# A backward-weight matmul with pair products: two more tiles taken as pairs, one accumulator set kept in three banks, closings and additions moved between engines

## The chip, the cores and the metric

The kernel runs on one core of a Trainium2 chip. The metric is the device time of one execution in microseconds; the median of three runs is given, and one further execution was profiled. In the profile PE is TensorE, PEld its weight loads, DVE VectorE, ACT ScalarE, POOL GpSimd and SP SyncE.

## The reference

```python
batch, m, k, n = 16, 512, 1024, 768
input:       (16, 512, 1024) float32
grad_output: (16, 512, 768)  float32
grad_weight = np.einsum('bmk,bmn->kn', input, grad_output)   # (1024, 768) float32
```

Seen as matrices, X is 8192 x 1024, G is 8192 x 768, and the output is X transposed times G: a contraction over 8192 rows.

## The kernel before

**Tiles.** The 8192 rows are 32 tiles of 256 rows, loaded one after another by POOL's queue (L152, L153; the first ones in halves, L157 and L159), with a conversion to bf16 on the way. Rows 0 to 127 of G and rows 0 to 255 of X come as float32 by SP's and ScalarE's queues and are rounded by VectorE and ScalarE (`round_by`, L199 to L217). `PAIRS_HELD` is the number of buffers that the tiles turn through, `SUMS_HELD` that of the sums below. All load instructions stand ahead of everything else that POOL does.

**Plain tiles and pairs.** `LOADS` says how each tile is used. The output is cut into four blocks: A (left columns, first half of k), B (right columns, first half), C (left, second half), D (right, second half), each of four row groups q = 0..3 of 128 x 384. A plain tile ("s") is two items of 128 rows; each item gives one matmul to each of the 16 groups, so a tile takes 32 matmuls. A pair tile ("P") is multiplied by a Winograd scheme for 2 x 2 blocks: seven products instead of eight, named 1, A, B, C, 5, 6 and 7, so 28 matmuls. The products need sums of the halves of X and of G: `sum_x` (L179, three VectorE operations) and `sum_g` (L189, three more), in the order written in the plan as x0.u, x1.u, x2.u and g0.u, g1.u, g2.u for tile u. At the end the shared products 1, 5, 6 and 7 are added into A, B, C and D (`SHARED`).

**Banks.** PSUM has eight banks of 512 float32 columns, and a group takes 384 of one bank. There are 32 groups (eight streams of four), so most groups are in PSUM only now and then. A group is *opened* by a matmul that starts it in a bank (`C3@5.1`: group C3 in bank 5, one matmul) or by a *fill* (`fD0@2`: ScalarE copies the group's sum so far from SBUF into the bank, L274). It is *closed* by ScalarE (`cC3`: copy to SBUF, L327) or VectorE (`vC2`: a copy, L329, or an addition to the sum in SBUF, L331, when the group was opened without a fill). The last closing of a group is done by VectorE and adds the shared product (L307 to L312), and the finished block is stored (L316 to L321), the first three in halves. A's four groups stay in banks 7, 3, 4 and 1 from start to end; banks 0, 2, 5 and 6 turn among all the others. The very last group, B3, is filled into two banks (`fB3@2+7`), as 256 and 128 columns.

**Order.** `PLAN` is one list, written out by hand or by a program outside the kernel, and the loop at L336 issues its tokens in that order. Each engine runs its own share of the list in order; what an engine waits for are the semaphores of the tiles that it touches. `WARMUP` (L133) is a handful of matmuls on constants ahead of the first data.

Of the kernel before, what the change touches and what calls it, by code (L numbers as in the profile page):

```python
# [9 lines left out]
P = 128  # L10

LOADS = "ssssssPPPPPPPPPPPPPPPPPPPPPPPPPs"

PLAN = (
    "A0@7.1 A3@3.1 A1@4.1 C3@5.1 C2@0.1 C1@2.1 r0 cC3 C0@6.1 vC2 A2@1.1 cC1 D0@5.1 vC0 B0@0.1 cD0 D1@2.1 "
    "r1 r3 B3@6.1 r2 D3@5.2 vB0 r4 A1.1 A2.1 cD1 vB3 A3.1 B1@0.2 cD3 B2@2.2 vB1 D2@6.2 cB2 C0@5.1 C1@0.1 "
    "vD2 A0.1 fD0@2 A2.1 vC0 A3.1 fD1@6 A1.1 D0.2 vC1 C2@5.2 cD0 D1.2 vC2 C3@0.2 cD1 B0@2.2 vC3 B3@5.3 "
    "fB1@6 vB0 A0.2 fB2@0 vB3 B1.2 fC0@2 B2.2 cB1 C1@5.2 vB2 C0.2 fD2@6 A3.1 vC1 D3@0.2 cC0 D2.2 fC2@5 "
    "vD3 C3@2.1 A1.1 cD2 A2.1 vC3 C2.1 B0@0.1 D1@6.1 vC2 D0@2.1 vB0 fD2@5 A3.2 vD1 A1.2 fB0@0 D2.2 vD0 "
    "B1@6.2 cD2 B0.2 vB1 B2@2.2 cB0 B3@5.2 vB2 C0@6.2 fC1@0 A2.2 vB3 fC2@2 C1.2 vC0 C3@5.2 cC1 C2.2 vC3 "
    "fD0@6 A0.2 D1@0.4 vC2 D3@5.4 vD1 D0.4 vD3 C3@2.2 vD0 B3@5.2 C0@0.2 vC3 fC1@6 A3.2 vB3 fB2@2 A0.2 vC0 "
    "C1.2 fD2@5 B2.2 cC1 D2.2 vB2 C2@0.2 cD2 B0@6.2 vC2 fB1@2 A1.4 vB0 fC1@0 B1.4 C2@5.2 cB1 D2@6.2 vC2 "  # L30
    "C1.2 fD0@2 A2.4 vD2 fD3@5 vC1 fC3@6 D0.2 D3.2 vD0 C3.2 cD3 C0@0.2 vC3 B2@2.4 vC0 fB3@6 B0@5.4 vB2 "
    "fD1@0 B3.4 fC0@2 vB0 A3.1 g0.6 fB1@5 A3.3 vB3 A0.2 g1.6 A0.2 fC1@6 D1.1 g2.6 D1.3 A2.2 vD1 A1.3 x0.6 "
    "fC2@0 C0.3 C1.1 x1.6 C1.2 cC0 C2.1 x2.6 C2.2 cC1 C3@2.1 g0.7 C3.2 cC2 B1.3 fD0@6 vC3 D2@0.2 g1.7 cB1 "
    "D0.2 vD2 fD3@2 A2.1 A3.1 A0.1 g2.7 cD0 10@5.1 D3.2 c10 x0.7 11@0.2 cD3 12@6.2 v11 13@5.2 c12 50@2.1 "
    "x1.7 50.1 c13 51@0.2 x2.7 52@6.2 c50 g0.8 53@5.2 c51 70@2.2 v52 c53 A2.1 g1.8 A3.1 fB3@0 72@6.2 v70 "
    "73@5.2 c72 g2.8 B3.2 v73 63@2.2 cB3 B2@6.1 x0.8 B2.1 fC1@5 A1.2 v63 A0.2 71@0.1 x1.8 71.2 vB2 62@2.3 "
    "c71 x2.8 C1.2 c62 g0.9 60@6.3 cC1 61@2.1 g1.9 61.2 fB0@0 v60 10@5.2 c61 g2.9 B0.3 v10 fC3@6 C2@2.2 "
    "cB0 x0.9 C2.1 C3.3 fC0@5 vC2 A2.2 f52@0 C0.1 x1.9 cC3 C0.2 A3.1 x2.9 A3.1 cC0 12@2.1 g0.10 12.1 52.2 "
    "f63@5 v12 B1@6.3 c52 g1.10 63.2 f13@2 vB1 11@0.2 c63 A0.1 g2.10 13.2 v11 72@5.2 c13 x0.10 A1.2 f51@0 "
    "53@6.2 v72 A0.1 f70@2 A3.1 51.1 x1.10 f50@5 51.2 v53 70.3 c51 x2.10 50.2 f73@6 g0.11 50.1 B3@0.3 c70 "  # L40
    "v50 73.2 fB2@2 g1.11 73.1 vB3 A2.1 f10@5 B2.2 c73 g2.11 B2.1 10.1 x0.11 10.2 cB2 C1@0.3 c10 x1.11 "
    "62@6.2 f71@2 vC1 A3.1 A1.1 f61@5 A0.1 x2.11 71.2 f60@0 g0.12 71.1 61.3 v62 c71 60.1 g1.12 60.2 c61 "
    "B0@2.1 g2.12 fB1@6 B0.2 v60 11@5.2 vB0 B1.2 fC0@0 A2.1 x0.12 A2.1 cB1 A0.1 C0.3 fC2@2 v11 A3.1 fC3@6 "
    "A1.1 x1.12 C2.3 cC0 x2.12 13@5.2 f53@0 g0.13 13.1 C3.3 cC2 v13 53.2 f52@2 g1.13 53.1 vC3 12@5.3 c53 "
    "g2.13 52.3 f72@6 v12 63@0.2 x0.13 c52 63.1 72.3 f62@5 v63 A2.1 f51@2 A1.1 x1.13 62.2 c72 51.1 x2.13 "
    "51.2 f50@0 v62 73@6.3 c51 g0.14 50.3 f70@5 v73 A3.1 fB2@2 A0.1 70.1 g1.14 c50 70.2 g2.14 B3@6.3 c70 "
    "B2.1 x0.14 B2.2 10@5.3 vB3 cB2 C1@0.1 x1.14 C1.2 f60@6 v10 11@2.3 x2.14 60.2 f61@5 g0.15 60.1 A1.1 "
    "61.3 c60 vC1 A0.1 g1.15 71@6.3 c61 v11 B0@0.1 fB1@5 g2.15 B0.2 v71 A2.2 fC2@2 A3.1 x0.15 A3.1 f52@6 "
    "B1.3 vB0 C2.2 cB1 x1.15 C2.1 52.2 cC2 x2.15 52.1 C0@0.1 fC3@5 g0.16 C0.2 A1.1 c52 A0.1 vC0 C3.3 "
    "f12@2 g1.16 13@6.3 vC3 12.2 g2.16 f62@5 12.1 v13 53@0.3 c12 x0.16 62.3 f72@6 A1.1 v53 63@2.3 c62 "  # L50
    "x1.16 f50@0 72.4 v63 f51@5 50.1 g0.17 50.2 c72 70@2.1 x2.16 70.2 c50 g1.17 51.3 v70 73@6.2 g2.17 c51 "
    "73.1 B2@0.1 x0.17 fB3@2 B2.2 A2.2 fC1@5 v73 B3.3 x1.17 C1.3 vB2 cB3 10@6.2 x2.17 cC1 10.1 71@0.1 "
    "g0.18 f11@2 71.2 A3.2 v10 f60@5 11.1 g1.18 11.2 v71 60.3 c11 g2.18 61@6.3 c60 x0.18 A0.3 fC0@2 v61 "
    "B1@0.3 fB0@5 x1.18 C0.3 fC2@6 vB1 B0.2 cC0 x2.18 B0.1 C2.1 g0.19 f12@0 C2.2 C3@2.3 cB0 vC2 12.2 "
    "f62@5 g1.19 12.1 vC3 A1.2 c12 53@6.1 g2.19 53.2 f52@2 x0.19 13@0.4 v53 A3.2 52.1 x1.19 f72@6 52.3 "
    "v13 62.2 x2.19 c52 62.2 g0.20 73@0.3 c62 g1.20 63@2.4 f51@5 v73 72.1 g2.20 72.2 fC1@0 v63 51.3 c72 "
    "x0.20 A2.3 c51 70@2.1 x1.20 70.3 f71@5 x2.20 50@6.4 v70 C1.1 g0.21 C1.2 fB2@2 A0.2 v50 cC1 B2.2 "
    "g1.21 B2.2 fB3@6 g2.21 A1.2 cB2 B3.4 x0.21 71.3 cB3 B0@0.2 x1.21 c71 B0.1 10@6.2 x2.21 10.2 vB0 "
    "C2@2.2 g0.22 C2.1 f61@0 A3.2 vC2 11@5.3 g1.22 11.1 f60@2 61.4 v10 g2.22 60.4 v11 c61 x0.22 C0@6.4 "
    "f53@0 c60 12@5.1 x1.22 12.3 vC0 B1@2.2 x2.22 B1.2 g0.23 C3@6.4 v12 53.2 g1.23 53.2 vB1 A1.2 c53 vC3 "  # L60
    "52@5.3 f73@2 g2.23 13@0.2 x0.23 13.2 A2.3 v52 A0.1 x1.23 A0.2 f51@5 v13 A3.2 51.1 x2.23 51.2 g0.24 "
    "51.1 73.3 c51 g1.24 73.1 C1@6.1 g2.24 C1.2 c73 63@5.4 vC1 f72@2 70@0.1 x0.24 f71@6 70.2 72.5 v63 v70 "
    "f62@5 A1.2 x1.24 c72 71.2 g0.25 71.2 f50@0 62.1 x2.24 fB2@2 62.2 g1.25 62.2 c71 B2.1 g2.25 B2.3 c62 "
    "50.4 vB2 B0@6.1 x0.25 f10@2 B0.3 c50 C2@5.1 x1.25 C2.3 f11@0 vB0 10.2 x2.25 10.2 g0.26 11.4 c10 vC2 "
    "B3@6.2 f60@2 g1.26 B3.2 c11 g2.26 B3.1 60.4 vB3 fB1@0 61@5.2 fC0@6 x0.26 61.2 c60 B1.4 v61 12@2.1 "
    "x1.26 fC3@5 12.3 vB1 C0.2 g0.27 f53@0 C0.2 x2.26 C3.2 cC0 g1.27 C3.2 v12 53.3 cC3 g2.27 53.1 52@6.4 "
    "v53 A2.1 x0.27 f51@0 A2.3 v52 A3.3 x1.27 A3.1 f70@6 A0.2 x2.27 A0.2 g0.28 A1.3 13@2.1 g1.28 13.2 "
    "g2.28 13.1 C1@5.4 v13 51.4 f73@2 vC1 70.1 x0.28 f63@5 70.3 c51 73.1 x1.28 73.3 c70 x2.28 73.1 63.2 "
    "c73 g0.29 63.3 f72@2 50@0.1 g1.29 50.2 c63 g2.29 50.1 71@6.4 v50 f62@5 72.4 fB0@0 v71 62.1 x0.29 "
    "f11@6 62.3 c72 B0.1 x1.29 B0.3 c62 x2.29 11.4 fB2@2 vB0 fC2@5 B2.1 g0.30 B2.4 f10@0 v11 C2.4 vB2 "  # L70
    "f11@6 10.1 g1.30 f12@2 10.3 vC2 A2.1 g2.30 A2.2 c10 x0.30 12.4 f13@5 f10@0 x1.30 11.1 13.3 c12 v11 "
    "10.1 A3.1 f61@2 x2.30 A3.2 v13 f62@6 A1.3 v10 f63@5 61.5 f60@0 62.2 v61 60.5 v62 f71@2 A2.2 f72@6 "
    "v60 A3.2 A1.2 vA2 f70@0 A0.5 vA3 vA1 70.3 vA0 63.2 v70 f50@1 71.2 72.2 fC0@3 v63 50.2 f73@0 v71 C0.6 "
    "f51@4 v72 fC1@5 v50 51.3 f52@2 fC2@7 C1.5 vC0 fD0@6 v51 fB0@1 52.4 fD1@3 B0.4 vC1 fB1@4 C2.3 v52 "
    "fD2@5 B1.7 vB0 fB2@2 vC2 73.2 vB1 B2.3 v73 f53@1 D0.2 D1.2 fC3@4 vB2 53.4 vD0 C3.6 vD1 v53 fD3@0 "
    "fB3@2+7 D2.2 D3.2 vC3 B3.7 vD2 vD3 vB3 "
).split()


WARMUP = [("b", 512), ("f", 512), ("f", 512), ("b", 512)]  # L80
PAIRS_HELD = 14
SUMS_HELD = 10

MERGED = 2


@with_exitstack
def kernel(
# [6 lines left out]
    nc = tc.nc  # L95
    bf16 = mybir.dt.bfloat16
    f32 = mybir.dt.float32
# [153 lines left out]


    SHARED = {"A": "1", "B": "5", "C": "7", "D": "1", "6": "1", "7": "6"}

    done = {(p, q): 0 for p in streams for q in range(Q)}
    fresh = {(p, q): True for p in streams for q in range(Q)}
    closed = set()
    opened = {}
    used = {7}
# [5 lines left out]
    def fill(p, q, b, b2):  # L265
        assert (p, q) not in opened and not fresh[p, q] and b in used
        src = sum_of(p, q)
        if b2 is None:
            parts = [(bank(b), 0, NH)]
        else:  # L270
            assert b2 in used
            parts = [(bank(b), 0, 256), (bank(b2), 256, NH)]
        for tile_, c0, c1 in parts:
            nc.scalar.copy(out=tile_[:, 0 : c1 - c0], in_=src[:, c0:c1])  # L274
        opened[p, q] = (parts, True)

    def multiply(p, q, b, n):
        first = (p, q) not in opened
        if first:
            opened[p, q] = ([(bank(b), 0, NH)], False)  # L280
            used.add(b)
        parts, carried = opened[p, q]
        for tile_, c0, c1 in parts:
            for j in range(n):
                at = done[p, q] + j
                stat, mov = operands(p, streams[p][at], q)
                nc.tensor.matmul(  # L287
                    tile_[:, 0 : c1 - c0],
                    stat,
# [7 lines left out]
    def close(engine, p, q):  # L297
# [34 lines left out]
        if final:  # L332
            closed.add((p, q))
# [51 lines left out]
```

## Time and profile before

| | us |
|---|---|
| median of 3 runs | 162.35 (162.25 to 162.43) |
| profiled execution | 162.31 |
| its span, first to last instruction | 160.5 |
| TensorE busy | 155.3, 937 instructions |
| VectorE busy | 142.7, 323 instructions |
| ScalarE busy | 112.8, 253 instructions |
| load queue (q0) | 28.64 MB, 90.2% of 16 engines' span |

The time is that of the whole execution; the span lies 1.8 us inside it. "Busy" is the time in which at least one of the engine's instructions ran. The instructions of one engine overlap in its pipeline, so what one of them costs is better read from the distance between two starts than from its own duration. Two lines give the sizes of the main copies; after the count stand the busy time, the mean duration in ns, and the idle time of the engine just before them:

```profile
L274 ACT COPY bank<-macc 128x384 f32<-128x384 f32 x71 | 33.6, 484 | 13.2 <-DVE macc L331 5.6
L327 ACT COPY macc<-bank 128x384 f32<-128x384 f32 x61 | 28.6, 479 | 9.5 <-PE bank L287 8.1
```

### The profile page before, as it was taken

To read this page: it belongs to the slowest core of one execution; us is meant where nothing else is said; L and a number is where in the kernel's file an instruction comes from. 1 tells how busy PE (TensorE), PEld (TensorE's weight loads), DVE (VectorE), ACT (ScalarE), POOL (GpSimd) and SP (SyncE) were. 2 spreads that over 40 slices of the span, in tenths; PEclk is the share of its full clock that TensorE was granted. 3 is DMA by queue.
4 is the path that set the end of the run, shared out by engine and by line. 5 is a ranking of instruction groups with operands and counts; after the bars stand their busy time and mean duration, and the time that the engine had idled before them with its cause. 6 is when DMAs were issued, how large, how long until landed. Compare 5 with 4: busy or idle time off the path is not lost.

```text
span 160.5 us, 2776 instructions
## 1 busy us (share of the span) xinstructions
PE 155.3 (97%) x937; PEld 91.9 (57%) x937; DVE 142.7 (89%) x323; ACT 112.8 (70%) x253; POOL 34.8 (22%) x69
## 2 busy tenths in 40 slices
PE   8899999999999999999999999999999999999990
PEld 3355556556556656655655655665665665556560
DVE  0788986989999999999989998998899998989992
ACT  3779737749888999968777786534777368877730
POOL 7452222122221222222122222212222100000000
PEclk9999999999999999999999999999999999999999
DMA  5999999999999999999999999999999999924385
GB/s 176 295 213 213 210 216 213 213 213 212 213 212 212 213 213 214 210 214 213 215 214 213 213 212 212 213 212 214 213 210 213 215 212 214 212 43 157 137 294 196
DMA packets 12830, 33.40 MB, mean 208 GB/s; under 512 B 1424, under 2 KB 4624, under 8 KB 12816
## 3 DMA queue, kind: packets, MB, share of 16 engines
q0 software_dynamic: 9360, 28.64, 90.2%
q1 hardware_dynamic: 3024, 3.47, 6.3%
q10 hardware_dynamic: 432, 1.11, 1.8%
q8 instruction: 7, 0.11, 0.3%
q14 instruction: 7, 0.06, 0.1%
HBM read 58.72 MB, written 3.15 MB: 385 GB/s over the span
## 4 chain that ended last, share of the span: by engine, by line
DMA 48%; PE 44%; DVE 2%; issue 2%; POOL 1%; DVEq 0%; POOLq 0%
DMA xp<-in_input_dram 48%; PE bank L287 44%; POOL gp L157 1%; DVE acc L312 1%; DVE xe L183 0%; POOL xp L159 0%; DVE acc L331 0%; DVE macc L331 0%; DVEq L380 0%; DVE xe L185 0%; POOLq L153 0%; POOLq L369 0%; POOLq L152 0%
## 5 line engine op out<-in xcount | busy, mean ns | idle before, releaser
L287 PE MATMUL bank<-gp,xp 128*128 128x384 bf16 (+2 forms) x631 | 109.8, 324 | 0.6 <-DVE xp L201 0.6
L287 PEld LDWEIGHTS <-xp 128*128 128x128 bf16 x631 | 61.1, 98 | 42.5 <-DVE xp L201 1.3
L287 PE MATMUL bank<-ge,xe 128*128 128x384 bf16 x300 | 56.2, 326 | 0.1
L274 ACT COPY bank<-macc 128x384 f32<-128x384 f32 x71 | 33.6, 484 | 13.2 <-DVE macc L331 5.6
L287 PEld LDWEIGHTS <-xe 128*128 128x128 bf16 x300 | 29.3, 98 | 19.9 <-issue 0.6
L274 ACT COPY bank<-acc 128x384 f32<-128x384 f32 (+1 forms) x70 | 32.3, 479 | 9.1 <-DVE acc L329 5.5
L327 ACT COPY macc<-bank 128x384 f32<-128x384 f32 x61 | 28.6, 479 | 9.5 <-PE bank L287 8.1
L331 DVE TENSOR_TENSOR acc<-bank,acc 128x384 f32<-128x384 f32 x54 | 28.7, 552 | 2.8 <-PE bank L287 1.2
L153 POOL DMA_DIRECT2D xp<-in_input_dram x30 | 16.0, 532 | 53.3 <-DMA xp<-in_input_dram 28.0
L327 ACT COPY acc<-bank 128x384 f32<-128x384 f32 x45 | 21.4, 480 | 6.5 <-PE bank L287 6.0
L152 POOL DMA_DIRECT2D gp<-in_grad_output_dram x30 | 16.0, 533 | 37.1 <-DMA gp<-in_grad_output_dram 15.0
L331 DVE TENSOR_TENSOR macc<-bank,macc 128x384 f32<-128x384 f32 x41 | 22.5, 551 | 0.5 <-PE bank L287 0.2
L183 DVE TENSOR_TENSOR xe<-xp 128x1024 bf16<-128x1024 bf16 x25 | 17.1, 683 | 1.2 <-DMA xp<-in_input_dram 1.2
L329 DVE COPY acc<-bank 128x384 f32<-128x384 f32 x24 | 13.1, 553 | 3.0 <-PE bank L287 2.4
L193 DVE TENSOR_TENSOR ge<-gp 128x768 bf16<-128x768 bf16 x25 | 13.8, 550 | 0.0
L187 DVE TENSOR_TENSOR xp<-xp,xe 128x512 bf16<-128x512 bf16 x25 | 10.5, 419 | 0.4
L185 DVE TENSOR_TENSOR xe<-xe,xp 128x512 bf16<-128x512 bf16 x25 | 10.5, 418 | 0.3
L197 DVE TENSOR_TENSOR gp<-ge,gp 128x384 bf16<-128x384 bf16 x25 | 8.8, 352 | 0.3
L195 DVE TENSOR_TENSOR ge<-gp,ge 128x384 bf16<-128x384 bf16 x25 | 8.7, 350 | 0.2
L312 DVE TENSOR_TENSOR acc<-bank,macc 128x384 f32<-128x384 f32 (+2 forms) x17 | 8.0, 522 | 0.0
L329 DVE COPY macc<-bank 128x384 f32<-128x384 f32 x14 | 7.6, 552 | 0.4 <-PE bank L287 0.4
L201 DVE CAST gp<-gf 128x192 bf16<-128x192 f32 (+1 forms) x2 | 0.7, 360 | 4.9 <-DMA gf<-in_grad_output_dram 4.9
(17 smaller groups left out, 21.6 us busy)
## 6 DMA issues: line engine op xcount, KB each, us to landing
xp<-in_input_dram POOLq DMA_DIRECT2D x30, 512.0 KB, 16.9
gp<-in_grad_output_dram POOLq DMA_DIRECT2D x30, 384.0 KB, 16.7
out_dram<-acc SPq DMA_DIRECT2D x12, 192.0 KB, 1.9
xf<-in_input_dram ACTq DMA_DIRECT2D x2, 512.0 KB, 5.0
gp<-in_grad_output_dram POOLq DMA_DIRECT2D x3, 192.0 KB, 6.6
out_dram<-acc SPq DMA_DIRECT2D x6, 96.0 KB, 1.7
xp<-in_input_dram POOLq DMA_DIRECT2D x2, 256.0 KB, 8.0
gf<-in_grad_output_dram SPq DMA_DIRECT2D x2, 192.0 KB, 4.2
```

Of the source, the lines that this page charges most:

```text
L152: nc.gpsimd.dma_start(out=gp, in_=G[rows, :].rearrange("(p m) n -> p m n", m=2))
L153: nc.gpsimd.dma_start(out=xp, in_=X[rows, :].rearrange("(p m) k -> p m k", m=2))
L183: nc.vector.tensor_sub(out=xe[:, 0:2, :], in0=x[:, 1::-1, :], in1=x[:, 3::-2, :])
L185: nc.vector.tensor_sub(out=xe[:, 2, :], in0=xe[:, 0, :], in1=x[:, 0, :])
L187: nc.vector.tensor_add(out=x[:, 1, :], in0=x[:, 2, :], in1=xe[:, 2, :])
L193: nc.vector.tensor_add(out=ge[:, 0:2, :], in0=g[:, 0:2, :], in1=g[:, 1::2, :])
L274: nc.scalar.copy(out=tile_[:, 0 : c1 - c0], in_=src[:, c0:c1])
L287: nc.tensor.matmul(tile_[:, 0 : c1 - c0], stat, mov[:, c0:c1], start=first and j == 0, stop=True, skip_group_check=True,)
L312: nc.vector.tensor_add(out=dst[:, c0:c1], in0=b, in1=sum_of(SHARED[p], q)[:, c0:c1])
L327: nc.scalar.copy(out=dst, in_=b)
L329: nc.vector.tensor_copy(out=dst, in_=b)
L331: nc.vector.tensor_add(out=dst, in0=b, in1=dst)
```

## The change

Two tiles that were plain are pairs now: four plain tiles first and one last, 27 pairs between. A's four groups of 384 columns are packed into three banks, 5, 6 and 7 (`@R` in the plan): A0 in bank 5, A1 as 128 columns in bank 5 and 256 in bank 6, A2 as 256 in bank 6 and 128 in bank 7, A3 in bank 7. Each matmul of A1 and A2 becomes two. Five banks, 0 to 4, turn among the other groups.

A group may now be open in two places at once, and ScalarE may close a group that was opened without a fill: it copies the partial sum to one of 16 places aside, and a later fill with an "s" at its end (`fC2@4s`) brings it back. There are 16 such closings. GpSimd does ten additions: `p` adds the shared product into a block's sum in SBUF ahead of its last closing (seven), `q` adds it after ScalarE has closed the block (three, A1 to A3) and then stores it. The order of all tokens is new; the warm-up is 512 columns and 32 matmuls of 128 columns; 11 tiles and 8 sums are held instead of 14 and 10; four stores go in halves; and the shared product of D is gathered in 6's place instead of 1's. `RESIDENT = 4` and `FOLDED = False` choose branches of the new code: the token `k` doesn't occur.

```diff
-LOADS = "ssssssPPPPPPPPPPPPPPPPPPPPPPPPPs"
+LOADS = "ssssPPPPPPPPPPPPPPPPPPPPPPPPPPPs"
 PLAN = (
-    "A0@7.1 A3@3.1 A1@4.1 C3@5.1 C2@0.1 C1@2.1 r0 cC3 C0@6.1 vC2 A2@1.1 cC1 D0@5.1 vC0 B0@0.1 cD0 D1@2.1 "
+    "A0@R.1 C1@0.1 C3@1.1 cC1 C2@2.1 r0 C0@3.1 vC3 A3@R.1 cC2 D0@4.1 B3@0.1 vC0 A2@R.1 cD0 B2@1.1 D1@2.1 r1 r3 "
...
-    "fB3@2+7 D2.2 D3.2 vC3 B3.7 vD2 vD3 vB3 "
+    "63.1 v10 63.2 p61 63.1 x2.30 60.1 f71@0 60.1 v63 60.1 f12@3 61@1.2 v60 61.1 f73@4 61.1 71.2 f51@2 p70 v61 "
+    "71.2 12.1 g2.30 12.1 v71 73.1 51.1 c12 51.1 v73 A0.1 fC1@0 A0.1 p62 A0.1 v51 70@1.1 f50@3 62@4.2 A1.3 v62 "
+    "A1.1 50.2 x2.28 cA1 50.3 f53@4 C1.1 vA0 qA1 C1.1 fD0@2 A3.2 v70 A3.1 fD3@5 A3.2 p72 v50 f52@1 C1.1 A2.3 "
+    "53.2 vC1 cA3 pC0 53.1 72@3.2 v53 cA2 D0.2 D3.1 qA3 D3.1 fB2@7 C0@0.2 v72 fB3@6 C0.3 vD3 fD2@3 C3@4.1 qA2 "
+    "C3.1 vD0 C3.3 vC0 52.1 fC2@2 B2.1 pB0 B2.1 v52 B2.1 fD1@5 B2.2 D2.2 pC3 B3.1 vB2 B3.3 vD2 B3.1 fB1@1+7 "
+    "D1.2 vB3 B0@0.3 vC3 B0.3 vD1 C2.3 vB0 C2.3 B1.2 vC2 B1.3 vB1 "
 ).split()
-WARMUP = [("b", 512), ("f", 512), ("f", 512), ("b", 512)]
-PAIRS_HELD = 14
-SUMS_HELD = 10
+WARMUP = [("b", 512)] + 32 * [("b", 128)]
+PAIRS_HELD = 11
+SUMS_HELD = 8
+HALVED = 4
+ASIDES = 16
+RESIDENT = 4
+FOLDED = False
...
+    def resident_parts(q):
...
+            resident.update({b: bank(b) for b in (5, 6, 7)})
+        a, b, c = (resident[i] for i in (5, 6, 7))
+        return [
+            [(a, 0, 0, NH)],
+            [(a, NH, 0, 128), (b, 0, 128, NH)],
+            [(b, 256, 0, 256), (c, 0, 256, NH)],
+            [(c, 128, 0, NH)],
+        ][q]
...
-    def fill(p, q, b, b2):
+    def fill(p, q, banks, from_aside):
         src = sum_of(p, q)
+        if from_aside:
+            slot = asides[p, q].pop(0)
+            free_asides.append(slot)
+            src = aside[:, slot, :]
...
-    def close(engine, p, q):
-        parts, carried = opened.pop((p, q))
+    def close(engine, p, q, queue):
+        parts, carried = opened[p, q].pop(0)
...
+        away = engine == "c" and not carried
+        if away:
+            asides[p, q].append(free_asides.pop(0))
+            dst = aside[:, asides[p, q][-1], :]
+        for tile_, at, c0, c1 in parts:
+            b = tile_[:, at : at + c1 - c0]
+            to = dst[:, c0:c1]
+            if engine == "c":
+                nc.scalar.copy(out=to, in_=b)
...
+            elif carried:
+                nc.vector.tensor_copy(out=to, in_=b)
+            else:
+                nc.vector.tensor_add(out=to, in0=b, in1=to)
...
+    def add_shared(p, q, prepare, queue):
+        dst = sum_of(p, q)
+        nc.gpsimd.tensor_add(out=dst, in0=dst, in1=sum_of(SHARED[p], q))
+        if prepare:
+            prepared.add((p, q))
+        else:
+            closed.add((p, q))
+            store(p, q, 0, NH, queue)
```

## The prediction

> **What bounds the kernel now.** I read the engine totals and the slices first, then the chain of waits, the busy times by stretch, the groups by form, and the timeline where a price was needed.
>
> ```profile
> PE 155.3 (97%) x937; PEld 91.9 (57%) x937; DVE 142.7 (89%) x323; ACT 112.8 (70%) x253; POOL 34.8 (22%) x69
> DMA  5999999999999999999999999999999999924385
> ...
> 84.41 70.98 PE bank L287 x435
> ...
> 45.00:55.00 10.00, 10.00 (x64) 5.99 (x62) 9.88 (x24) 9.34 (x23) 2.65 (x5) 1.00 1.07 212
> 55.00:65.00 10.00, 10.00 (x63) 6.04 (x62) 9.90 (x25) 9.30 (x22) 2.51 (x5) 1.00 1.07 213
> 105.00:115.00 10.00, 10.00 (x64) 6.01 (x62) 9.52 (x23) 4.64 (x11) 2.52 (x5) 1.00 1.07 213
> ```
>
> TensorE is busy in 97% of the span, and from 84.41 us to the end of matmuls the chain is TensorE alone. The stretches (PE, PEld, DVE, ACT, POOL in that order) show what lies close under it: VectorE has 9.9 of 10 us in the middle, ScalarE 9.3 there and 4.6 later, and the DMAs run without a pause until about 142 us. So the bound is TensorE, with VectorE and the loads right behind, and ScalarE the one engine with room.
>
> The first real matmul starts at 5.19 us and the last at 156.64. The starts between them hold ten gaps that are wider than one matmul, together 1.27 us over the pitch: 0.47 us up to 7.6 us (the first casts and bank turns), 0.28 us up to 16 us (a tile lands), 0.3 us at 83.9 (the chain names the pair's sum L183 there, after a landing), the rest 0.2 us. Everything else is matmuls back to back.
>
> ```profile
> 155.54 0.82 PE L287 MATMUL bank<-gp,xp 128*128 128x256 bf16 x6
> ...
> 156.09 0.60 PE L287 MATMUL bank<-gp,xp 128*128 128x256 bf16 x6
> 156.31 0.55 PE L287 MATMUL bank<-gp,xp 128*128 128x128 bf16 x7
> ...
> 156.53 0.33 PE L287 MATMUL bank<-gp,xp 128*128 128x128 bf16 x3
> ```
>
> Prices come from starts, not from durations, since a matmul's listed 326 ns overlaps the next ones. From 155.54 to 156.09 lie five starts of 256 columns: 0.11 us each (0.109 in the starts themselves). From 156.31 to 156.53 lie four of 128 columns: 0.055 us each, with a weight load before each one. A matmul of 384 columns starts 0.1625 us after the one before.
>
> ```profile
> 47.43 0.48 ACT L327 COPY acc<-bank 128x384 f32<-128x384 f32 x1
> 47.80 0.49 ACT L274 COPY bank<-acc 128x384 f32<-128x384 f32 x1
> 48.22 0.49 ACT L274 COPY bank<-macc 128x384 f32<-128x384 f32 x1
> ...
> 59.99 0.55 DVE L331 TENSOR_TENSOR acc<-bank,acc 128x384 f32<-128x384 f32 x1
> 60.46 0.68 DVE L183 TENSOR_TENSOR xe<-xp 128x1024 bf16<-128x1024 bf16 x1
> 61.06 0.55 DVE L331 TENSOR_TENSOR macc<-bank,macc 128x384 f32<-128x384 f32 x1
> ```
>
> In the same way a ScalarE closing takes 0.376 us (47.43 to 47.80), a fill 0.415 (47.80 to 48.22), a VectorE closing 0.466 (59.99 to 60.46), the first sum of a pair 0.60. Every VectorE operation starts 0.08 us before its forerunner's listed end, so the six sums of a pair (0.683, 0.418, 0.419, 0.550, 0.350, 0.352 in the groups, 2.77 together) take 2.77 - 6 x 0.08 = 2.29 us.
>
> **The change part by part.** *Matmuls.* Two tiles turn from plain (32 matmuls) into pairs (28): 924 become 916, which is 8 x 0.1625 = 1.30 us less. The packing of A cuts each of the 37 matmuls of A1 and of A2 into 128 + 256 columns: 0.055 + 0.109 = 0.165 against 0.1625, so 74 cuts cost 74 x 0.0025 = 0.19 us. The last block is cut as before (5 matmuls instead of 7). Net: 1.30 - 0.19 = 1.1 us less on TensorE. The bounds of a cut: 0.0025 us by the row above; at worst its weight load is not hidden and the narrow matmul takes 0.098 us, the load's mean, 0.043 more. I take the row: seven in a row ran so at the end, each with its load. The Trainium skill's "TensorE: Matmul & The Clock Gate", section Back-to-back issue gap, gives about 81 ns for a sustained stream of loads and matmuls of 128 columns; by it the cuts would cost some 1.9 us more and eat the gain, but the trace's 55 ns disagree, if only on seven matmuls.
>
> *VectorE.* Two more pairs add 2 x 2.29 = 4.6 us. Its closings, counted in the two orders, go from 166 operations to 160: 6 x 0.466 = 2.8 us less. So 1.8 us more on an engine with some 18 idle us, of which about 8 lie in the start and the end. Sixteen openings that VectorE would have added go out by ScalarE to a place aside and come back later as a fill.
>
> *ScalarE.* Fills go from 141 to 169, closings from 106 to 148: 28 x 0.415 + 42 x 0.376 = 27.4 us more, 113 to 140. That is the change's real price, and it isn't even. From the first sum x0.4 to x0.14 the new order holds 264 matmuls (43.0 us), 46 fills and 64 closings (43.2 us of ScalarE), and 42 closings and ten pairs' sums (42.2 us of VectorE); from x0.4 to x0.22 it is 77.3 us of TensorE against 76.8 of ScalarE. Today's busiest stretch, x0.6 to x0.14, has 34.3 of TensorE to 28.3 and 31.6. Three engines are therefore loaded to 98 to 100% for some 40 us, two of them for 77. A fourth joins: the loads' packets, counted in order, show tile 4 landed at 25.1 us, 14 at 68.7, 22 at 103.2, a tile each 4.32 us, and the new order reaches x0.18 to x0.24 about 0.35 us nearer to the landing than today's. What covers it: five banks turn instead of four, so from a bank's last matmul to the next tenant's first after a fill, the order leaves a median of 2.3 us where it left 1.8 (VectorE closings: 2.4, was 2.1). I put the new stalls at 0.5 us: the 0.35 for the landings and 0.15 for the loaded engines. Bounds: nothing, as VectorE at 9.9 of 10 costs TensorE nothing today, or below nothing by 0.2 (the mid gaps vanish through the fifth bank); above, see the first rival.
>
> *GpSimd.* The ten additions stand behind POOL's last load in program order, which was issued at 125.6 us. Seven of them, qA1 to pC3, lie within 47 matmuls (7.6 us) ahead of vC3, which needs the last of them: 1.09 us each before anything is late. The trace has no such operation; below stands POOL's memset of 0.10 us, above the longest single operation off TensorE and the queues, 1.28 us (the table load). Nearest is the same addition on VectorE, 0.55; I take no cost, and 7 x 0.19 = 1.3 us as the upper end. Queued behind qA1 on SP are the later stores, none of which ends the span.
>
> *Buffers, start, end.* With 11 tiles held instead of 14, load u waits for the use of tile u-11: the tightest, tile 20 for load 31, is used up at about 110 us by the order, and that load was issued at 125.6; cover 15 us, cost nothing. Eight sums held: pair 29 writes at 131 us what pair 21 left at 120. The warm-up (0.78 to 4.63 us today, followed by 0.56 us of waiting for the first cast) becomes 512 columns and 32 x 128. The first warm-up row took 0.38 us per 512 columns, so 32 x 0.095 = 3.0 us more, done near 4.4; if each load of 0.128 us is not hidden, 32 x 0.22 = 7.1 us, 3 us late, less the 0.28 us wait up to 16 us. I take nothing. The second matmul now waits for the third cast (+0.2 us), and the wait for the right half of the first G tile, at 6.3 us today, comes two matmuls earlier; the tile that TensorE awaits at 16 us covers both. The tail (last matmul start to last VectorE end, 156.64 to 157.39) is a queue of VectorE closings in both: the same within 0.1.
>
> *Sum.* The profiled execution took 162.31 us (span 160.5 and 1.8 around it), 0.04 below the median. 162.31 - 1.1 + 0.5 = 161.7 us.
>
> **The rivals.** *ScalarE decides (slower).* From x0.4 to x0.22 it has 194 copies and 0.5 us to spare. Each 10 ns that a copy loses on average to a wait cost 1.9 us; the wider turns absorb about 0.5. It eats the gain from (1.1 + 0.5)/194 = 8 ns on; at 15 ns TensorE waits 2.9 - 0.5 = 2.4 us: 163.6 us. For it: ScalarE waits now and then today (0.33 us at 51.8 us, for TensorE), and its 9.3 of 10 was never tried at 10. Against it: VectorE runs at that load.
>
> *The loads and the even pace eat the gain (same).* If x0 waits for each landing and TensorE follows, up to 1.1 us goes: 162.3. Against: each pair brings 28 x 0.1625 = 4.55 us of matmuls to 4.32 of loading, and work left over grows.
>
> *GpSimd ends last (slower).* At 1.28 us each vC3 is 1.3 us late, five closings behind it: 163.0. The Trainium skill's "GPSIMD Engine Reference", section 3.1, has the addition at 1.96 times VectorE's time, an estimate of 1.08 us from the 0.55 here, right at the limit; no row shows it.
>
> *Narrow matmuls wait for weights (slower).* 74 x 0.043 = 3.2 us: 164.9.
>
> **How the numbers follow.** Forecast 0.50, with 161.0 (no stall, 0.2 gained) to 162.0 as its own range; the even pace 0.14 (162.3); ScalarE 0.21 (162.4 to 164, a quarter of it within the 0.2%); GpSimd 0.09; narrow matmuls or warm-up 0.06. A run of this kernel can tell 0.2%, 0.32 us, from no change. Faster 0.50, same 0.14 + 0.06 = 0.20, slower 0.30. The range from 161.0 to 163.4 leaves out the narrow matmuls and the upper third of ScalarE's case.
>
> **What would show it.** Right: 995 real matmuls with starts 0.055 us apart after A's 128 columns; first to last start near 150.8 us instead of 151.45; ScalarE at 9.8 or more of 10 from 30 to 100 us while PE stays at 9.9; POOL additions below 1.09 us. Wrong: PE below 9.8 in those stretches with fills or closings named as releasers; x0 waiting for landings with PE idle beside it; the chain of waits ending on POOL; pitches above 0.08 at the cuts.

## The result, and the profile after

| | us |
|---|---|
| before, median of the four runs on the same chip | 162.30 (162.23 to 162.43) |
| after, median of four runs | 163.87 (163.27 to 163.94) |
| ratio after to before | 1.0087 (95%: 1.0071 to 1.0104) |
| after, profiled execution and its span | 163.89 and 162.12 |

The change makes the kernel slower by 0.9%. The forecast was 161.7 us; the time lies above the range.

Two rows of the page after answer to those shown of before, the engines' totals and the DMA slices:

```profile
PE 154.8 (95%) x1028; PEld 97.4 (60%) x1028; DVE 144.8 (89%) x329; ACT 133.2 (82%) x325; POOL 44.6 (28%) x79
...
DMA  5999999999999999999999999999999999901595
```

The busy stretches (PE, PEld, DVE, ACT and POOL after the length; then the granted clock, the DMA share, GB/s):

```profile
45.00:55.00 10.00, 10.00 (x65) 6.08 (x64) 9.91 (x25) 10.00 (x27) 2.64 (x5) 1.00 1.06 210
85.00:95.00 10.00, 10.00 (x69) 6.25 (x67) 9.47 (x23) 10.00 (x26) 2.19 (x5) 1.00 1.07 212
...
135.00:145.00 10.00, 9.53 (x59) 5.53 (x57) 9.93 (x20) 5.10 (x12) 2.94 (x3) 1.00 0.67 133
145.00:155.00 10.00, 9.75 (x67) 6.25 (x67) 9.77 (x22) 6.69 (x18) 6.88 (x8) 1.00 0.38 125
```

In the middle, ScalarE is busy without a pause, as worked out, and TensorE stands at 10 beside it. Of these rows, only the last two show a loss: PE 9.53 and 9.75, just where POOL, idle at that point before, begins to work. The same two rows of the kernel before have PE at 10.00 in both:

```profile
135.00:145.00 10.00, 10.00 (x63) 5.92 (x62) 8.99 (x21) 8.11 (x20) 0.00 (x0) 1.00 0.66 133
145.00:155.00 10.00, 10.00 (x63) 6.05 (x62) 10.00 (x23) 7.07 (x17) 0.00 (x0) 1.00 0.56 196
```

The chain of waits after names who is late there:

```profile
1.18 5.71 DMA gf<-in_grad_output_dram
...
7.33 132.42 PE bank L338 x875
...
140.32 0.56 DVE macc L385
140.88 0.21 DVE xp L195
...
141.97 0.56 DVE macc L378
...
142.54 0.96 ACT bank L316 x2
...
143.54 0.50 PE bank L338 x2
...
144.19 1.02 DVE macc L378 x2
...
145.25 11.90 PE bank L338 x82
```

Before, TensorE alone stood on the chain from 84.41 us on. Now it begins with the second half of the first G tile, which lands at 6.89 us (the first row), leaves TensorE at 139.7, passes through a sum of the last pair (L195, x2.30), VectorE's closings and a fill, and comes back at 145.25.

The spans differ by 162.12 - 160.54 = 1.58 us. From the starts of the matmuls and the landings of the stores:

| part | us |
|---|---|
| first real matmul later (5.19, now 5.27) | +0.07 |
| matmul work | -1.12 |
| gaps between matmuls up to 10 us | +0.66 |
| gaps from 10 to 139 us | -0.15 |
| gaps behind 139 us | +1.0 |
| last matmul to VectorE's end | +0.03 |
| VectorE's end to the last store's landing (1.77, now 2.56) | +0.79 |
| last landing to the end of the span | +0.3 |

So the 1.1 us of matmul work did go, and came back as gaps, and the stores added about a microsecond. What the sum can't say is whether the matmuls would have been worth anything without those gaps. That takes the experiments.

### The profile page after: what moved, and what is told of

Read it like the earlier page. It is cut to its first block, busy times and chain, and to the rows that moved or that the text cites. A ratio compares the mean times of both kernels' runs of the same rounds, so it can differ in the third digit from the quotient of the medians.

```text
span 162.1 us, 3067 instructions
## 1 busy us (share of the span) xinstructions
PE 154.8 (95%) x1028; PEld 97.4 (60%) x1028; DVE 144.8 (89%) x329; ACT 133.2 (82%) x325; POOL 44.6 (28%) x79
## 3 DMA queue, kind: packets, MB, share of 16 engines
q10 hardware_dynamic: 432, 1.11, 1.9%
## 4 chain that ended last, share of the span: by engine, by line
PE 89%; DMA 4%; DVE 2%; issue 1%; ACT 1%; DVEq 0%; SPq 0%; ACTq 0%
PE bank L338 89%; DMA gf<-in_grad_output_dram 4%; DVE macc L378 1%; ACT bank L316 1%; DVE macc L385 0%; ACT macc L363 0%; DVEq L451 0%; SPq L135 0%; DVE gp L209 0%; DVE xp L195 0%; DVE acc L378 0%; DVEq L378 0%; DVEq L371 0%; ACTq L363 0%
## 5 line engine op out<-in xcount | busy, mean ns | idle before, releaser
L338 PEld LDWEIGHTS <-xp 128*128 128x128 bf16 x671 | 63.0, 98 | 38.1 <-DVE xp L209 1.1
L338 PE MATMUL bank<-ge,xe 128*128 128x384 bf16 x324 | 63.9, 326 | 0.7 <-DVE macc L378 0.6
L316 ACT COPY bank<-macc 128x384 f32<-128x384 f32 x89 | 43.3, 511 | 6.3 <-DVE macc L385 4.4
L363 ACT COPY macc<-bank 128x384 f32<-128x384 f32 x77 | 37.1, 515 | 3.4 <-PE bank L338 3.0
L385 DVE TENSOR_TENSOR acc<-bank,acc 128x384 f32<-128x384 f32 x56 | 30.2, 555 | 1.5 <-PE bank L338 0.9
L363 ACT COPY acc<-bank 128x384 f32<-128x384 f32 (+2 forms) x57 | 26.6, 485 | 5.4 <-PE bank L338 5.1
L385 DVE TENSOR_TENSOR macc<-bank,macc 128x384 f32<-128x384 f32 x47 | 25.9, 558 | 1.0 <-PE bank L338 0.6
L383 DVE COPY macc<-bank 128x384 f32<-128x384 f32 x20 | 11.1, 554 | 1.9 <-PE bank L338 1.0
L195 DVE TENSOR_TENSOR xp<-xp,xe 128x512 bf16<-128x512 bf16 x27 | 12.3, 454 | 0.4
L316 ACT COPY bank<-aside 128x384 f32<-128x384 f32 x16 | 8.6, 552 | 0.0
L383 DVE COPY acc<-bank 128x384 f32<-128x384 f32 x14 | 7.6, 550 | 1.0 <-PE bank L338 1.0
L395 POOL TENSOR_TENSOR macc<-macc 128x384 f32<-128x384 f32 x4 | 4.1, 1027 | 15.7 <-ACT macc L363 14.4
```

Source lines behind the costliest of these rows:

```text
L195: nc.vector.tensor_add(out=x[:, 1, :], in0=x[:, 2, :], in1=xe[:, 2, :])
L316: nc.scalar.copy(out=tile_[:, at : at + c1 - c0], in_=src[:, c0:c1])
L338: nc.tensor.matmul(tile_[:, at : at + c1 - c0], stat, mov[:, c0:c1], start=fresh, stop=True, skip_group_check=True,)
L363: nc.scalar.copy(out=to, in_=b)
L383: nc.vector.tensor_copy(out=to, in_=b)
L385: nc.vector.tensor_add(out=to, in0=b, in1=to)
```

## The experiments

**e1_warmup.** The changed kernel with the old warm-up.

```diff
-WARMUP = [("b", 512)] + 32 * [("b", 128)]
+WARMUP = [("b", 512), ("f", 512), ("f", 512), ("b", 512)]
```

> The changed kernel with the warm-up of before (512 bf16, two of 512 float32, 512 bf16), nothing else. Theory: with the 32 narrow matmuls the TensorE clock was granted at 6.03 us instead of 3.93, and the first three real matmuls cost 0.34, 0.30 and 0.23 us instead of 0.16; with the old warm-up the clock is granted near 3.9, these 0.3 to 0.6 us come back, and the time is 163.2 to 163.6 us instead of 163.87. The order at the end stays as it was: about 1.1 us of TensorE gaps between 140 and 146 us. Rival (the even pace: tiles that land set the start anyway): the gain is lost again by 16 us, the time stays at 163.8 to 163.9.

164.11 us, ratio 1.0093 (1.0073 to 1.0113). The time does not fall, so the warm-up is not the cause. The profiled execution, the fastest of the six at 163.49, can't test the start by itself: its clock was granted at 6.67 us, even later than the changed kernel's 6.03, and not near 3.9 as expected. Its gaps up to 10 us are 0.42 us shorter, as the second half of the first G tile landed at 6.14 us and not at 6.89, and its first sum of the last pair (x0.30) started at 138.92 against 139.21 us, 0.29 earlier.

**e2_three_adds_dve.** The three additions p61, p70 and p62 by VectorE.

```diff
-        nc.gpsimd.tensor_add(out=dst, in0=dst, in1=sum_of(SHARED[p], q))
+        adder = nc.vector if (p, q) in [("6", 1), ("7", 0), ("6", 2)] else nc.gpsimd
+        adder.tensor_add(out=dst, in0=dst, in1=sum_of(SHARED[p], q))
```

> The changed kernel with three of the ten additions (p61, p70, p62) done by VectorE instead of GpSimd, at the same places of the order. Theory: GpSimd's additions, at about 1.0 us each, hold VectorE's bf16 sums that run at the same time (x2.30 took 1.24 us instead of 0.41 beside the one at 140.8 us, g2.30 0.91 instead of 0.35 beside the one at 143.1); without them both go back to 0.41 and 0.35, the TensorE gaps of 1.1 us between 140 and 146 us shrink below 0.4 although VectorE gets 3 x 0.55 us of new work, and the time falls by 0.5 to 1.0 us, to 162.9 to 163.4. Rival (three engines at 98 to 100 per cent have fallen behind by then and the end pays for it): moving more work to VectorE makes the gaps wider, 164 us or more. Second rival (the additions are merely waited for, no holding): x2.30 stays long.

164.19 us, 1.0118 (1.0097 to 1.0139): no gain. But the cause of the stall at 141 us shows. First VectorE's timeline of the changed kernel (start, duration), then POOL's, then VectorE's of this one:

```profile
140.32 0.56 DVE L385 TENSOR_TENSOR macc<-bank,macc 128x384 f32<-128x384 f32 x1
140.80 1.24 DVE L195 TENSOR_TENSOR xp<-xp,xe 128x512 bf16<-128x512 bf16 x1
...
142.90 0.54 DVE L385 TENSOR_TENSOR macc<-bank,macc 128x384 f32<-128x384 f32 x1
143.36 0.91 DVE L205 TENSOR_TENSOR gp<-ge,gp 128x384 bf16<-128x384 bf16 x1
```

```profile
140.76 0.99 POOL L395 TENSOR_TENSOR macc<-macc 128x384 f32<-128x384 f32 x1 [14.43 <-ACT macc L363]
143.05 2.07 POOL L395 TENSOR_TENSOR macc<-macc 128x384 f32<-128x384 f32 x2 [1.30 <-DVE macc L378]
```

```profile
141.04 0.42 DVE L195 TENSOR_TENSOR xp<-xp,xe 128x512 bf16<-128x512 bf16 x1
143.37 0.35 DVE L205 TENSOR_TENSOR gp<-ge,gp 128x384 bf16<-128x384 bf16 x1
...
146.56 1.12 DVE L195 TENSOR_TENSOR xp<-xp,xe 128x512 bf16<-128x512 bf16 x1
```

GpSimd's first addition runs from 140.76 to 141.76; x2.30 starts beside it at 140.80 and ends at 142.04, after the addition, in 1.24 us instead of 0.42. The second (the first of the two in POOL's second row) runs from 143.05 to 144.05; g2.30 ends at 144.27, in 0.91 instead of 0.35. A closing with a PSUM operand (L385) keeps 0.54 to 0.56. Without the three additions both sums are short, but x2.28, which now falls beside qA1, is held for 1.12, and VectorE has three operations more. The gaps moved to 143.77 (0.77 us) and 148.62 (0.95).

**e3_a_by_dve.** A1 to A3 closed by VectorE, which adds the shared product as the other blocks' closings do; qA1 to qA3 go.

```diff
-cA1 ... qA1 ... vC1 cA3 ... cA2 ... qA3 ... qA2
+    ... vA1 ... vC1 vA3 ... vA2
```

> The changed kernel with A1, A2 and A3 closed by VectorE with the addition of the shared product, as A0 is, instead of a ScalarE copy and a GpSimd addition (three GpSimd additions and five ScalarE copies less, five VectorE operations more). Theory: SP's first stores waited for GpSimd (from 147.98 to 151.82 us only six of the 20 stores went out) and the other 14 then followed one another each 0.49 us, so that the last one left 0.4 to 0.6 us after its data was ready; with A's blocks finished by VectorE the last store leaves within 0.1 us of its closing, and the stretch from the last VectorE operation to the last landing falls from 2.56 us to about 1.9. TensorE's gaps stay. Time 163.1 to 163.5. Rival: the stores are limited by the transfers (0.53 us per 192 KB), not by SP's waiting: then the end stays at 2.4 to 2.6 us after the last closing and the time within 0.2 of 163.87.

164.07 us, 1.0104 (1.0087 to 1.012). The stores were less late (the last landed 2.06 us after VectorE's end, not 2.56), but VectorE ended at 158.53, 0.66 us later. What SP gains, VectorE pays.

**e4_all_three.** e1, e2 and e3 together.

> The changed kernel with the three edits of the other runs together: old warm-up, three additions on VectorE, A closed by VectorE. Theory: the three losses lie behind one another and add up, so that what is left is the gain in matmuls of 1.1 us less some tenths: 161.3 to 162.2 us, below or at the kernel before. Rival (one common cause, a late stage that is too full for VectorE): the edits don't add up, 163 us or more.

164.89 us, 1.0151 (1.0134 to 1.0168), the slowest of these: VectorE ends at 158.73, with about 18.8 us of its own work from x0.30 on (about 16 in the changed kernel) and 0.9 us of waits. My parts don't add up, since they all put work on VectorE in a stage where it has nothing to spare.

**e5_order.** The additions stay on GpSimd. The three sums that can meet them move away from them: two ahead, x2.30 behind v51.

```diff
-x1.28 ... g1.30 ... p61 63.1 x2.30 ... 12.1 g2.30 12.1 ... v51 ... 50.2 x2.28 cA1
+x1.28 x2.28 ... g1.30 g2.30 ... p61 63.1 ... 12.1 12.1 ... v51 x2.30 ... 50.2 cA1
```

> The changed kernel with three sums at other places of the order and nothing else: x2.28 right behind x1.28, g2.30 right behind g1.30 (both ahead of the first GpSimd addition), x2.30 right behind v51, where GpSimd stands idle. Theory: a GpSimd addition holds a bf16 sum of VectorE until it ends, and from the last pair's first sum on VectorE has no time to spare, so the 0.83 + 0.56 us that x2.30 and g2.30 lost are lost at the end. Both now take 0.41 and 0.35 us, VectorE's work stays the same, the TensorE gaps between 140 and 146 us fall from 1.1 us to below 0.5, and the time falls by 0.6 to 1.2 us to 162.7 to 163.3. Rival (the late stage is too full for VectorE in any order): the gaps move to another place and the time stays within 0.3 us of 163.9.

163.34 us, 1.0061 (1.004 to 1.0081). The sums take 0.35 to 0.42 again. From 140 to 146 us, the changed kernel first, then this one:

```profile
140.00:146.00 6.00, 5.28 (x36) 3.09 (x34) 5.97 (x11) 3.82 (x9) 3.06 (x3) 1.00 0.23 46
```

```profile
140.00:146.00 6.00, 5.96 (x42) 3.68 (x41) 5.65 (x12) 4.04 (x11) 2.99 (x3) 1.00 0.20 40
```

POOL works about as long, TensorE gets back 0.68 us, and VectorE does one operation more in less busy time. VectorE ends at 157.50 instead of 157.87, so the held sums cost about 0.4 us of the end by these two profiles. This one has an accident of its own: tile 20's landing was signalled at 95.80 us (95.07 in the changed kernel), and TensorE has 0.47 us of gaps behind it. Not all of the gaps are gone, either: a new one of 0.37 us stands at about 133 us, in e6 and e9 too.

**e6_order_store.** e5, with SP also bound to the list's order, and the store of A2, whose addition ends late, behind pC3.

```diff
-    ctx.enter_context(tc.manual_schedule(engines={E.PE, E.DVE, E.Activation, E.Pool}))
+    ctx.enter_context(tc.manual_schedule(engines={E.PE, E.DVE, E.Activation, E.Pool, E.SP}))
-C3@4.1 qA2 ... pC3
+C3@4.1 ... pC3 qA2
```

> The kernel with the three moved sums, and SP's stores held to the order of the list, with A2's GpSimd addition and its store moved behind pC3 (before, A1's and A2's stores waited for GpSimd ahead of blocks that were done). Theory: SP no longer stands still while finished blocks wait, so the last store leaves within 0.15 us of its closing instead of 0.6 us later and the last landing follows the last VectorE operation by 1.8 to 2.1 us instead of 2.56: 0.4 to 0.7 us less than the run with the moved sums alone. Rival (the transfers limit, 0.53 us per store of 192 KB): no difference above 0.2 us.

162.89 us (twelve runs), 1.0037 (1.0017 to 1.0056). VectorE ended at 157.01 us, 0.38 earlier than in the kernel before; tile 20 was not late here (95.04). The last landing still came 2.31 us after that: 192 KB stores land 0.535 us apart at best, so what SP's queue holds back late runs back to back to the end.

**e7_idle_adds.** The kernel before, with eight GpSimd additions of 128 x 384 float32 on a tile that nobody uses, behind x0.28.

```diff
+    if token == "x0.28":
+        nc.gpsimd.memset(idle, 0.0)
+        for _ in range(8):
+            nc.gpsimd.tensor_add(out=idle, in0=idle, in1=idle)
```

> The kernel of before with eight GpSimd additions of 128 x 384 float32 on a tile of their own that nothing else uses, behind POOL's last load (about 126 to 135 us). Theory: they hold VectorE's bf16 sums (x and g of pairs 28 and 29) though nothing waits for their results: those that start during an addition take 0.5 to 0.9 us longer than their 0.35 to 0.68, VectorE's closings beside them (float32 with one operand in PSUM) keep 0.55, each addition takes 1.0 to 1.1 us, and the time rises to 164 to 167 us. Rival (the long x2.30 and g2.30 waited for a result): all sums keep their times and the kernel stays at 162.1 to 162.8.

165.44 us in one execution, against 162.23 for the kernel before. POOL's row, then VectorE's:

```profile
126.68 6.56 POOL L342 TENSOR_TENSOR idle<-idle 128x384 f32<-128x384 f32 x7
```

```profile
126.34 0.55 DVE L332 TENSOR_TENSOR macc<-bank,macc 128x384 f32<-128x384 f32 x1
126.81 0.97 DVE L186 TENSOR_TENSOR xe<-xe,xp 128x512 bf16<-128x512 bf16 x1
127.81 0.93 DVE L188 TENSOR_TENSOR xp<-xp,xe 128x512 bf16<-128x512 bf16 x1
128.67 1.17 DVE L194 TENSOR_TENSOR ge<-gp 128x768 bf16<-128x768 bf16 x1
129.88 0.86 DVE L196 TENSOR_TENSOR ge<-gp,ge 128x384 bf16<-128x384 bf16 x1
130.78 0.87 DVE L198 TENSOR_TENSOR gp<-ge,gp 128x384 bf16<-128x384 bf16 x1
131.57 0.55 DVE L332 TENSOR_TENSOR macc<-bank,macc 128x384 f32<-128x384 f32 x1
```

Nothing waits for these additions and they wait for nothing, so this is the disturbance alone. Each of the five bf16 sums beside them takes 0.5 to 0.6 us more than it does elsewhere (0.42, 0.42, 0.55, 0.35, 0.35), and so do the next two, up to 134.8 us; the closings with a PSUM operand don't change. TensorE has gaps of 1.99 us at 130.5 and 0.51 at 133.2, and x0.30 starts 3.0 us late.

**e8_act_copies.** The changed kernel with twelve ScalarE copies of 128 columns, at x0.8 to x0.19.

```diff
+    if token in ['x0.8', 'x0.9', ... 'x0.18', 'x0.19']:
+        nc.scalar.copy(out=idle[:, 0, :], in_=idle[:, 1, :])
```

> The changed kernel with twelve more ScalarE copies of 128 columns, one at each x0 from pair 8 to pair 19, on a tile of their own (each some 0.2 us, 2.4 us in all between 43 and 92 us). Theory: ScalarE at 10.0 of 10 us there is loaded exactly to what TensorE lets it and has no reserve, so TensorE's gaps between 40 and 100 us rise from 0.3 us to 1.5 to 2.4. Rival (the busy share counts waiting that would give way, five banks leave a reserve): the gaps stay below 0.6 us.

166.07 us in one execution; 163.87 is the changed kernel's median. TensorE's gaps from 40 to 100 us grew from 0.25 to 2.24 us. The same stretch as above:

```profile
85.00:95.00 10.00, 9.78 (x62) 5.79 (x61) 8.94 (x22) 10.00 (x27) 2.30 (x5) 1.00 1.07 213
```

ScalarE at 10 of 10 has no reserve there: with these copies added, TensorE waits. As the change has it, the fit is just good enough.

**e9_stores_early.** e5, with SP in the list's order, A3's store right behind its closing, A2's behind the last vC0, and no halved stores.

```diff
-... vC1 cA3 pC0 ... D3.1 qA3 ... C3@4.1 qA2 ... vC0 52.1
+... vC1 cA3 qA3 pC0 ... D3.1 ... C3@4.1 ... vC0 qA2 52.1
-HALVED = 4
+HALVED = 0
```

> The kernel with the three moved sums and SP in the order of the list; A3's GpSimd addition goes right behind its closing and A2's right behind C0's last closing, and no store is cut in halves (16 places instead of 20 on SP). Theory: VectorE ends at 157.0 us already, 0.4 us before that of the kernel before, and what is left is that the 3 MB of stores start 3.5 us later than there and run one after another at 0.53 us each until 159.3; each finished block that goes out earlier shortens that row. The last landing follows the last VectorE operation by 1.7 to 2.0 us instead of 2.3; time 162.0 to 162.5 us, level with the kernel before. Rival (the row is set by when VectorE's closings come): the last landing stays 2.3 us behind and the time at 162.9.

162.04 us (twelve runs), 1.0001 (0.9984 to 1.0019): level with the kernel before. VectorE ends at 157.50 as in e5, with the same late tile 20, and the last landing comes 1.6 us after it (in e5: 2.5). The stretch from 145 to 155 us of e5, then of this one (last figure GB/s):

```profile
145.00:155.00 10.00, 10.00 (x71) 6.38 (x69) 9.69 (x21) 6.38 (x17) 7.30 (x8) 1.00 0.42 139
```

```profile
145.00:155.00 10.00, 10.00 (x71) 6.38 (x69) 9.69 (x21) 6.38 (x17) 7.36 (x8) 1.00 0.48 172
```

The engines do the same work within 0.06 us; only the stores moved more in it: 172 GB/s against 139, and 125 in the changed kernel (196 before). Three things differ from e5 at once: SP's order, the places of two additions, and 16 issues on SP instead of 20. Which of them did how much is not separated.

**e10_eight_mid and e11_eight_last.** Two experiments on the kernel before, to price eight matmuls on their own: A0's and A1's on four tiles in the middle (tiles 12, 14, 16, 18) are left out; or the last two of each group of A on the last tile.

```diff
+        if p == "A" and q < 2 and items[streams[p][at]][1] in (12, 14, 16, 18):
+            continue
```

> The kernel of before without eight of its 924 matmuls: A0's and A1's on tiles 12, 14, 16 and 18 are left out (the output lacks these products). Theory: between 30 and 138 us the first sum of each pair is paced by its landing, so TensorE only stands still 1.3 us longer, and what follows the last pair's first sum (116 matmuls, 17.6 us of VectorE) is the same: the time falls by 0 to 0.3 us. Rival (the view of the prediction: TensorE bounds, each matmul off it is 0.1625 us off the time): 1.2 to 1.3 us less, 161.0.

```diff
+        if p == "A" and streams[p][at] >= len(items) - 2:
+            continue
```

> The kernel of before without eight other matmuls, the last two of each of A's four groups, on the last tile (the output lacks these products), all of them behind the last pair's first sum. Theory: VectorE has 17.6 us of closings and sums behind that first sum and 1.0 us of waits, TensorE 17.7 us; with TensorE 1.3 us shorter VectorE can give up no more than its waits: 0.3 to 0.9 us less. Rival (TensorE alone bounds): 1.2 to 1.3 us less.

e10: 162.27 us, 1.0000 (0.999 to 1.001). e11: 162.30 us, 1.0009 (1.0000 to 1.0017). Eight matmuls, 1.30 us of TensorE, are worth nothing in either place of that kernel. The busy stretch of e10 where they go, then that of e11:

```profile
65.00:75.00 10.00, 9.87 (x62) 5.84 (x60) 9.93 (x24) 8.23 (x19) 2.64 (x5) 1.00 1.06 211
```

```profile
135.00:145.00 10.00, 9.25 (x57) 5.41 (x56) 9.01 (x21) 8.13 (x20) 0.00 (x0) 1.00 0.66 133
```

In e10 x0.30 starts at 138.61, only 0.17 us earlier than before. Part of the 1.30 us is lost at the start of this execution (gaps of 1.09 us up to 10 us against 0.47, with the clock granted at 6.74 us), and from 60 to 100 us TensorE waits 0.72 us against 0.35. The first sums show why nothing is left: x0.18 to x0.29 start 0.02 to 0.11 us after their tile's landing is signalled, against 0.02 to 0.37 before, so what TensorE saves is waited out at the next landing. In e11 it waits 0.91 us for a fill at 143.4, and VectorE ends at 157.40 as before (157.39).

**e12_change_again.** The changed kernel once more, on the chip of e9 to e11.

> The changed kernel once more, beside the others on the same chip. Both theories: 163.3 to 164.0 us, with the gaps of 1.1 us between 140 and 146 us and x2.30 at 1.24 us; the late landing of the second half of the first G tile at 6.57 us (5.6 to 5.8 in all other profiles) doesn't come back, as nothing in the change touches it.

163.74 us, 1.0102 (1.0087 to 1.0116): the changed kernel's loss stands, with the same held sum (1.24 us for x2.30). Here the gaps up to 10 us are 0.44 us, as in the kernel before (0.47), and the second half of the first G tile was signalled at 6.16 us. So the 0.66 us at the start was an accident, the late landing of that tile half (last packet 6.57 us, signalled at 6.89); e8's profile has it once more (6.67 and 6.99). Without it the span is only 0.12 us shorter: gaps from 10 to 139 us are 1.01 us instead of 0.56.

## Why the prediction was wrong

**The step that failed first: "So the bound is TensorE", and with it the term of -1.1 us.** The size was right: 995 real matmuls, 1.12 us less work. Its worth was not: in the kernel before, e10 and e11 give 0 for 1.30 us, ahead of x0.30 and behind it. Ahead of x0.30 the landings set the pace (tile 30 landed at 137.77 us before, 138.06 after and 137.87 in e10; x0.30 started about 1.0, 1.15 and 0.74 us later), and the list fixes which matmuls stand behind it. Behind x0.30 VectorE is full: from that start to its end it takes 18.61 us before, about 17.6 of them its own work (39 operations), and e11, with 1.30 us less of TensorE there, leaves its end at 157.40 (157.39).

The changed kernel has 116 matmul instructions behind x0.30, as before, but more of them are pieces: 90 of 384 columns, and 13 cut into 256 and 128 (before: 102 and 7). That is about 16.8 us of TensorE instead of 17.7, so most of the saving lies here. VectorE has 36 operations, about 16 us of its own. Yet the stretch is 18.66 us, as 2.7 are lost, half of them by the next step. So from first to last start the matmuls took 151.82 us, where I had 150.8. The two rows of VectorE's timelines from which I count:

```profile
138.78 0.68 DVE L183 TENSOR_TENSOR xe<-xp 128x1024 bf16<-128x1024 bf16 x1
```

```profile
139.21 0.69 DVE L191 TENSOR_TENSOR xe<-xp 128x1024 bf16<-128x1024 bf16 x1
```

TensorE at 10 of 10 was a busy engine, not the one that set the end: VectorE and the loads stood as close. The chain of waits did give a warning, in the half that the prediction does not show. TensorE stands on it alone for the last 71 us; up to 82.4 us it lies on the loads, as the profile's page of before sums up:

```profile
DMA 48%; PE 44%; DVE 2%; issue 2%; POOL 1%; DVEq 0%; POOLq 0%
```

The rival "the loads and the even pace eat the gain", at 162.3, named half of this; e9, with the two losses below made smaller, is there, at 162.04 and a ratio of 1.0001. Whether some of the gain would come out without any loss is open: e6's VectorE ended 0.38 us earlier than before, and its stores used that up.

**"I take no cost" for GpSimd, the second step that failed.** I asked whether the additions would be in time (1.09 us each allowed, 0.99 to 1.11 measured), and priced only the seven ahead of vC3. I did not ask what they do to an engine beside them. The Trainium skill's "GPSIMD Engine Reference", section 8, says that GpSimd and VectorE share their SBUF interfaces, and contend when VectorE runs certain fast modes or reads two operands from SBUF. The runs agree for the bf16 sums, which read two: 0.42 becomes 1.24 us, and in e7 0.93 and 0.97; closings with one operand in PSUM, which are float32 besides, keep 0.55; no run separates the two. The hold costs x2.30 0.83 and g2.30 0.56, 1.39 us of VectorE in its full stage, and 1.04 us of gaps in TensorE. e5, with the sums moved, is at 1.0061 where the changed kernel is at 1.0087 and 1.0102, which makes the hold some 0.4 to 0.7 us of the time (each ratio has some 0.2% each way). "GpSimd ends last" had the place right, and not the way.

**"Queued behind qA1 on SP are the later stores, none of which ends the span": the third step that failed.** The last store's landing came 0.79 us later behind VectorE's end than before. SP's issues, before and then after, and the row of SP's waits after (us in total, times, longest):

```profile
144.35 13.41 SPq L320 DMA_DIRECT2D out_dram<-acc  x19
```

```profile
147.98 10.72 SPq L298 DMA_DIRECT2D out_dram<-acc  x20
SPq L298 <- POOL acc L395: 146.4, 1, 146.4
```

The stores begin 3.6 us later, and most of that is the new order: the first finished block is ready at 147.52 us, against 144.32 before. SP's first store waits for a GpSimd addition (qA1, which ends at 147.95), 0.43 us more: SP isn't among the engines that follow the list, where A0 stands first. The view shows no later store that stands still for GpSimd.

Then SP stands still once more: its sixth issue takes 1.53 us (150.29 to 151.82; the others at most 0.44), and after a landing at 150.09 none is signalled until 152.56. Beside it the instruction queue q8 moves a packet of 16 KB, from 150.05 to 151.45 us. e3, with no addition of A1 to A3 on GpSimd, has the same stall (packet to 151.88, issue to 152.24), and e10, without any GpSimd addition, too. So GpSimd is not its cause, though A2's addition ends at 151.78 and its store might have stood there anyway. In the kernel before, the stall falls on the second store (packet to 145.08, issue to 145.47), with 12 us left to make it up. I had no term for this, and no run was aimed at it.

From 151.9 us on 14 stores leave SP without a pause, 0.49 us each to issue; the last is issued at 158.29, 0.6 us after its closing ended, and lands at 160.43. Keeping SP in the list's order and changing what is sent when took 1.0061 (e5) to 1.0037 (e6) and to 1.0001 (e9, whose stall was 0.64 us where e5's was 1.51). These two and e5 lie on two chips and have intervals of some 0.2% each way, so the share of each repair is less certain than their sum; e9 and e12, on one chip, differ by 1.0102 - 1.0001, about 1.6 us, for the hold and the stores together.

**The sum with what was measured.** In place of -1.1 for the matmuls stands 0, in place of +0.5 for new stalls 0, in place of nothing for GpSimd 0.4 to 0.7, and in place of nothing for the stores about 1.0 (e5 to e9): from 162.30 that gives 163.7 to 164.0 us, and 163.87 was measured.

**"New stalls at 0.5 us", and ScalarE's rival.** The middle cost nothing: gaps from 10 to 139 us were 0.56 us, 0.15 less than before (1.01 in e12, which had no late start). The load that I counted was right (ScalarE at 10.00; its closings are 150 instructions and not 148, as A1's and A2's go in two pieces), and e8 shows the cliff behind it, but the order stays on the safe side.

**Matmuls of 128 columns.** The rival fell: the 79 starts behind them have a median of 0.056 us, with a weight load each, as the seven rows before had it. The 81 ns that the Trainium skill's "TensorE: Matmul & The Clock Gate" gives in its section Back-to-back issue gap is not seen here, in a stream that mixes 128 columns with 256 and 384.

**"I take nothing" for the start.** Right in effect (the times of e1 and e12). **The tail "the same within 0.1".** Right for VectorE (0.75 and 0.78 us from last matmul to its end); the stores behind it were the miss.

What stays open is the 0.3 us between the last landing and the end of the span, which no run was aimed at. It belongs to the kernel and not to one execution: 1.35 to 1.39 us in the four profiles with the stores of before, 1.66 to 1.70 in the nine with 20 issues on SP, 1.50 in e9.

## What to carry to other kernels

An engine at 10 of 10 need not be the bound while another, or the loads, stand at 9 or more: read the chain of waits to its start, find the last thing that arrives from outside, count each engine's own work behind it, and price a saving by what lies behind that point; leaving out the few instructions in question is a cheap test. Before moving additions to GpSimd, look at what VectorE reads beside them, in a stage where VectorE is full above all. When blocks finish in another order, follow the store queue in its own order, from the first finished block to the last landing, and read from its own row of waits what it waits for.

## What the runs showed of the hardware

- A VectorE sum of two bf16 operands in SBUF that meets a GpSimd addition ends 0.2 to 0.4 us after the addition does (142.04 after 141.76, 144.27 after 144.05; in e7 too); sums of float32 with an operand in PSUM run on at 0.55 us.
- One such addition takes 0.99 to 1.12 us with two tiles (once 1.19, in e2), 0.82 to 1.15 in place on one tile.
- In 11 of the 14 profiles one issue of a store on SP ends 0.36 to 0.39 us after a 16 KB packet of the instruction queue q8, and has stood for 0.64 to 1.75 us; other issues take some 0.4.
- TensorE showed gaps of only 0.25 us together from 40 to 100 us, with ScalarE busy for 59.89 and VectorE for 58.57 of the 60 us.
- Full clock was granted anywhere between 3.64 and 6.74 us in 14 profiles: 3.64 to 6.03 with the new warm-up (median of eight 4.4), 3.93 to 6.74 with the old (median of six 6.1). The time does not follow it: e12, at 3.64, took as long as the changed kernel's profile, at 6.03.
- Stores of 192 KB landed 0.535 us apart: 192 x 1024 bytes in 0.535 us are 367 GB/s, and the page after has 368 GB/s in the slice that holds them.
